# Two plain pairs instead of three at each feed forward entry, with the streams' sums made kind by kind

## The chip, the core and the metric

The kernel runs on one core of one Trainium2 chip. The metric is the device time of one execution in microseconds (us). The engines are named as in the profile: PE is TensorE (its weight loads are PEld), DVE is VectorE, ACT is ScalarE, POOL is GpSimd, SP is SyncE.

## The reference, cut to what matters

A decoder trunk of four layers works on 512 prompt tokens and 8 times 8 sample tokens. Each layer has a token mixer (attention, a gated recurrence, a short convolution, attention) and then a feed forward block:

```
xp = xp + swiglu(rmsnorm(xp, norm_ffn[i]), ffn_w_gate[i], ffn_w_up[i], ffn_w_down[i])
def swiglu(h, wg, wu, wd):
    return (jax.nn.silu(h @ wg) * (h @ wu)) @ wd
```

The model width is 1024 (8 row blocks of 128, numbered m or k), the feed forward width 2816 (22 column blocks of 128). All arithmetic is at float32 accuracy.

## The kernel before, in words

The 576 tokens are held transposed as two **streams** g = 0 and 1 of 288 columns each. A product at float32 accuracy is made of three matmuls over split operands: high weight times high data, high times low, low times high (`mm3`, lines 439 to 441). "Splitting" a tile is an ACT cast into the high part and a DVE subtraction for the low part: lines 412 and 414 (and 359 and 361) for weights, lines 468 and 470 for data. The split normed stream is `hh`, `hl`; the split input of the second matrix is `mh`, `ml`.

The 22 column blocks of a feed forward layer lie in three segments of 8, 7 and 7. In each segment the gate and up products of its blocks are made first, then the part of the down product (`out_units`) that they feed. A block's gate and up weights are a **pair**, and a pair is multiplied in one of two ways:

- **plain**: four units (gate and up, for both streams). A unit is 8 row blocks times 3 matmuls, so a plain pair is 96 matmuls. Its evacuation is a SiLU on ACT (line 1334) and a product on DVE (line 1343), then a data split.
- **quad** (`quad`): the two weights and the two streams are taken as a 2 by 2 block product with seven half-size products instead of eight. Each product is 4 row blocks times 3 matmuls (lines 1367 to 1369), so a quad is 84 matmuls. The products come in the order A11, A12, S2, S1, S3, S4, A22. A11 and A12 multiply the halves of stream 0; S4 the second half of stream 1; S2, S1, S3 and A22 multiply the data sums **T2, T1, T3 and T4**, which are sums of the halves of both streams. S3 can only add into its bank after a copy of the bank (`snap`, line 1375) has gone to a scratch tile, and S4 after another one.

The first `PRE` = 3 pairs of a layer are plain, since the data sums are not there yet; the five further pairs of the first segment and all of the other two are quads.

The **data sums** are made by `tsums(k)`, for k = 0 to 3, from blocks k and k+4 of both streams: five DVE operations (line 1322) and four data splits. Each `tsums(k)` first takes one scratch tile, and gives three back after its last split (`b12`, `b22` and its own). The scratch pool `scr` has `NSCR` = 10 tiles. `hsplit` (line 494 makes the normed block, then a split) takes one for each of the eight blocks of stream 1 and keeps it until `tsums` gives it back. The statistics of a stream (line 600), the SiLU tiles and the quads' copies take theirs from the same pool.

The **weight sums** of a quad (S1 to S4, lines 378, 381, 384 and 388) are made on DVE for the first `NEAR` = 2 quads of a layer and on POOL for the later ones; there is one set of sum tiles (`NSTP` = 1), which a quad holds until all its weights are split. `qprep` splits the seven weight halves one after the other into halves of `NSLOT` = 6 weight slots.

The order of the work on every engine is fixed when the program is built: `Sched` plays the tasks through with assumed costs, and on each engine takes the ready task of the lowest priority number (not an operation that is not ready yet). Priorities count in weight tiles. With i0 for the number of a layer's first gate weight: units of stream 0 have i0, i0+1, ...; units of stream 1 the same plus 3.5; a quad that begins at weight i has i + 1.75; a weight's split has i − 1 (each later half of a quad 2/7 more); a quad's weight sums i − 1.1; a stream's split that of its statistics (i0 + 2.5 for stream 1); `tsums(k)` has i0 + 2.6 + 0.1 k. Each stream has its own list of units, in which a unit begins only when the one before it has been issued; the quads go alternately into the two lists.

Of the kernel before, what the change touches and what calls it, by code (L numbers as in the profile page):

```python
# [14 lines left out]
D = 1024  # L15
# [3 lines left out]
T = 8  # L19
# [7 lines left out]
N = NP + NS  # L27
# [6 lines left out]
LAG = 3  # L34
NSLOT = 6
NRAW = 4
PRE = 3
NEAR = 2
NSTP = 1
TOFF = 2.6  # L40
# [209 lines left out]
def cD(n, ap=0):  # L250
    return n / 960 + 0.07 + 0.06 * ap


class Builder(Sched):
# [38 lines left out]
    def add(self, g, fn):  # L293
        self.units[g].append((self.vidx(g), fn))
        self.nunits[g] += 1
# [996 lines left out]
    def ffn(self, layer):  # L1292
# [7 lines left out]
        T = {}  # L1300
        mixed = self.mixed

        def enter():
            yield ("wait", mixed)
            self.open(f"{layer}f")
            for n in ("T2", "T1", "T3", "T4"):
                T[n] = tuple(self.lt(n + s, [P, hk, N], F32R) for s in "hl")
            self.stp = Pool([tuple(self.lt(f"S{j}{i}", [P, HW]) for j in range(2)) for i in range(NSTP)])
            self.b11 = [self.lt(f"b11{i}", [P, N]) for i in range(hk)]
            self.qseen = []  # L1310
            yield ("set", ("ffnlp", layer))

        def tsums(k):
            yield ("wait", [("h", g, idx, m) for g in range(2) for m in (k, k + hk)])
            b11, b12, b22 = (self.whole.pop(gm) for gm in ((0, k), (1, k), (1, k + hk)))
            hh, hl = (a[:, k + hk, :].bitcast(F32) for a in self.h[0])
            [t4] = yield ("acq", self.scr, 1)
            sub, add = nc.vector.tensor_sub, nc.vector.tensor_add
            for n, t, x, y, op in (("T1", b11, b12, b11, sub), ("T3", b12, b22, b12, sub), ("T2", b22, b22, b11, sub),
                                   (None, t4, hh, b22, sub), ("T4", t4, t4, hl, add)):  # L1320
                yield ("D", cD(N))
                op(t, x, y)

            def parts(n, t):
                yield from self.split(T[n][0][:, k, :], T[n][1][:, k, :], t, N, 1)
            for n, t in (("T1", b11), ("T3", b12), ("T2", b22), ("T4", t4)):
                yield ("spawn", parts(n, t), None, [("T", layer, n, k)])
            yield ("wait", [("T", layer, n, k) for n in ("T1", "T3", "T2", "T4")])
            yield ("free", self.scr, [b12, b22, t4])

        def gate_evac(g, key, ps):
            [t] = yield ("acq", self.scr, 1)
# [106 lines left out]
        def start_quad(prio, i, s, m, lst):  # L1439
            self.open_quads += 1  # L1440
            return quad(i, s, m, lst)

        self.spawn(enter(), 0.0, 0.0)
        for k in range(hk):
            self.spawn(tsums(k), self.nunits[1] + TOFF + 0.1 * k, 0.0)
        for s, (_, ns) in enumerate(SEGS):
            pre = PRE if s == 0 else 0
            for m in range(ns):
# [227 lines left out]
```

## Time and profile before

| | us |
|---|---|
| median of 3 runs | 2353.8 (2353.73 to 2353.94) |
| the profiled execution, its own time | 2353.24 |
| its span, first to last instruction | 2351.3 |
| PE busy | 2324.0 (99%) |
| DVE busy | 1672.2 (71%) |
| ACT busy | 1226.6 (52%) |
| POOL busy | 542.6 (23%) |

The span is what the views of the profile divide up. The profiled execution took 1.94 us more than its span, and stands 0.56 us below the median. In the views, times within the span are counted from its start, and a line such as L1322 is line 1322 of the kernel before.

### The profile page before, as it was taken

The numbers are of one execution on the slowest core, as the hardware profiler recorded it, in microseconds if no ns is written. First come the engines' busy times: TensorE is split into PE (matmuls) and PEld (weight loads), VectorE is DVE, ScalarE is ACT, GpSimd is POOL, SyncE is SP. The second block draws the span as 40 slices with busy tenths as digits, with TensorE's granted clock in tenths as the row PEclk, the third lists the DMA queues.
The fourth block names the chain that finished last, engine by engine and source line by source line (L and its number), as shares of the span: only waits on it lengthen the run. The fifth ranks groups of instructions, "written<-read, shape, count | busy, mean of one in ns | idle before, by whom it ended". The sixth has DMA issues, their size and how long they took to land.

```text
span 2351.3 us, 44296 instructions
## 1 busy us (share of the span) xinstructions
PE 2324.0 (99%) x17596; PEld 2295.5 (98%) x17596; DVE 1672.2 (71%) x3315; ACT 1226.6 (52%) x2545; POOL 542.6 (23%) x636
## 2 busy tenths in 40 slices
PE   9999999999999999999999999999999999999998
PEld 8899999999999999999999999999999899999998
DVE  8978848486886885848665578484868959757474
ACT  8955625255695653525422256252548945535353
POOL 2300334240231033323000003242402400333330
PEclk9999999999999999999999999999999999999999
DMA  5111323233222132323322213232242111323131
GB/s 189 61 57 47 112 87 99 73 101 102 72 82 93 52 122 66 113 72 101 97 85 82 83 55 98 93 98 81 88 138 83 56 46 54 126 73 110 62 109 49
DMA packets 64064, 203.69 MB, mean 87 GB/s; under 512 B 11041, under 2 KB 13905, under 8 KB 63841
## 3 DMA queue, kind: packets, MB, share of 16 engines
q1 hardware_dynamic: 62800, 199.52, 26.7%
q8 instruction: 138, 2.26, 0.4%
q10 hardware_dynamic: 720, 0.73, 0.1%
q0 software_dynamic: 336, 0.61, 0.1%
q14 instruction: 70, 0.57, 0.1%
HBM read 197.87 MB, written 4.94 MB: 86 GB/s over the span
## 4 chain that ended last, share of the span: by engine, by line
PE 86%; ACT 6%; DVE 4%; issue 2%; DMA 1%; POOL 0%; DVEq 0%; ACTq 0%
PE bank L439 16%; PE bank L440 16%; PE bank L441 16%; PE bank L1367 12%; PE bank L1369 12%; PE bank L1368 12%; ACT s L753 2%; ACT wh L359 1%; DVE P L841 1%; PE bank L890 1%; PE bank L906 1%; ACT P L847 0%; DVE P L855 0%; ACT PT L892 0%; DVE wl L361 0%
## 5 line engine op out<-in xcount | busy, mean ns | idle before, releaser
L439 PE MATMUL bank<-mh,wh 128*128 128x288 f32 x1984 | 589.2, 297 | 1.7 <-ACT mh L468 1.7
L440 PE MATMUL bank<-ml,wh 128*128 128x288 f32 x1984 | 586.0, 295 | 0.5 <-DVE ml L470 0.4
L441 PE MATMUL bank<-mh,wl 128*128 128x288 f32 x1984 | 583.7, 294 | 0.0
L439 PE MATMUL bank<-hh,wh 128*128 128x288 f32 x1344 | 404.1, 301 | 4.1 <-ACT s L1123 1.5
L440 PE MATMUL bank<-hl,wh 128*128 128x288 f32 x1344 | 397.3, 296 | 0.0
L441 PE MATMUL bank<-hh,wl 128*128 128x288 f32 x1344 | 396.3, 295 | 0.0
L414 DVE TENSOR_TENSOR wl<-raw,wh 128x512 fp32r<-128x512 f32 x380 | 375.9, 1011 | 22.8 <-ACT wh L412 22.6
L359 ACT CAST wh<-raw 128x1024 fp32r<-128x1024 f32 (+2 forms) x217 | 219.0, 1014 | 326.0 <-PE bank L440 213.1
L439 PEld LDWEIGHTS bank<-mh,wh 128*128 128x128 f32 x1984 | 371.9, 187 | 3.4 <-ACT mh L468 2.5
L440 PEld LDWEIGHTS bank<-ml,wh 128*128 128x128 f32 x1984 | 372.5, 188 | 1.8 <-DVE ml L470 1.3
L441 PEld LDWEIGHTS bank<-mh,wl 128*128 128x128 f32 x1984 | 373.7, 188 | 0.0
L361 DVE TENSOR_TENSOR wl<-raw,wh 128x1024 fp32r<-128x1024 f32 (+2 forms) x217 | 256.7, 1183 | 65.9 <-ACT wh L359 64.0
L655 DVE TENSOR_TENSOR x<-bank,x 128x288 f32<-128x288 f32 x224 | 101.9, 457 | 280.1 <-PE bank L441 279.9
L412 ACT CAST wh<-raw 128x512 fp32r<-128x512 f32 x380 | 229.5, 619 | 95.2 <-PE bank L440 94.6
L1367 PE MATMUL bank<-hh,wh 128*128 128x288 f32 x912 | 270.0, 296 | 0.0
L1368 PE MATMUL bank<-hl,wh 128*128 128x288 f32 x912 | 269.1, 295 | 0.0
L1369 PE MATMUL bank<-hh,wl 128*128 128x288 f32 x912 | 268.2, 294 | 0.0
L439 PEld LDWEIGHTS bank<-hh,wh 128*128 128x128 f32 x1344 | 252.5, 188 | 6.7 <-ACT s L1123 1.7
L440 PEld LDWEIGHTS bank<-hl,wh 128*128 128x128 f32 x1344 | 253.1, 188 | 0.8
L441 PEld LDWEIGHTS bank<-hh,wl 128*128 128x128 f32 x1344 | 253.7, 189 | 0.1
L1384 ACT ACTIVATE s<-s 128x288 f32<-128x288 f32 x152 | 67.8, 446 | 216.7 <-DVE s L1380 215.6
L1369 PEld LDWEIGHTS bank<-hh,wl 128*128 128x128 f32 x912 | 171.9, 188 | 0.0
(382 smaller groups left out, 4863.9 us busy)
## 6 DMA issues: line engine op xcount, KB each, us to landing
raw<-in_w SPq DMA_DIRECT2D x303, 512.0 KB
raw<-in_w SPq DMA_DIRECT2D x64, 448.0 KB
out_y<-x SPq DMA_DIRECT2D x12, 144.0 KB
x<-in_x SPq DMA_DIRECT2D x4, 288.0 KB
x<-in_x SPq DMA_DIRECT2D x2, 576.0 KB
ck<-in_ckt SPq DMA_DIRECT2D x4, 256.0 KB
cv<-in_cv SPq DMA_DIRECT2D x4, 256.0 KB
ca<-in_ca SPq DMA_DIRECT2D x2, 480.0 KB
```

Of the source, the lines that this page charges most:

```text
L359: self.nc.scalar.copy(fh[:, z], r[:, z])
L361: self.nc.vector.tensor_sub(fl[:, z], r[:, z], fh[:, z].bitcast(F32))
L412: self.nc.scalar.copy(fh, src)
L414: self.nc.vector.tensor_sub(fl, src, fh.bitcast(F32))
L439: mm(out, lhsT=wh(k), rhs=xh(k), start=(k == 0), stop=False)
L440: mm(out, lhsT=wh(k), rhs=xl(k), start=False, stop=False)
L441: mm(out, lhsT=wl(k), rhs=xh(k), start=False, stop=(k == n - 1))
L655: nc.vector.tensor_add(x[:, m, :], ps[:, :N], x[:, m, :])
L1367: mm(ps[:, :N], lhsT=wh[:, k, :], rhs=xh[:, k, :], start=first and k == 0, stop=False, skip_group_check=not first)
L1368: mm(ps[:, :N], lhsT=wh[:, k, :], rhs=xl[:, k, :], start=False, stop=False, skip_group_check=not first)
L1369: mm(ps[:, :N], lhsT=wl[:, k, :], rhs=xh[:, k, :], start=False, stop=k == hk - 1, skip_group_check=not first)
L1384: nc.scalar.activation(out=t, in_=t, func=AF.Silu)
```

## The change

`PRE` becomes 2, so that in each of the four layers the third pair is a quad; the first segment then has two plain pairs and six quads. In `tsums` the same five operations and four splits are issued in another order and with other priorities: T1 and T2 of a block first, and all work of a kind is ranked by kind (T2's splits, T1's, T3, T4) before it is ranked by block. The scratch tile is now taken for T2, and T4 is made in `b22`.

```diff
-PRE = 3
+PRE = 2
@@ tsums
-            [t4] = yield ("acq", self.scr, 1)
+            [t2] = yield ("acq", self.scr, 1)
             sub, add = nc.vector.tensor_sub, nc.vector.tensor_add
-            for n, t, x, y, op in (("T1", b11, b12, b11, sub), ("T3", b12, b22, b12, sub), ("T2", b22, b22, b11, sub),
-                                   (None, t4, hh, b22, sub), ("T4", t4, t4, hl, add)):
-                yield ("D", cD(N))
-                op(t, x, y)
+            rank = lambda z: tprio + 0.08 * z + 0.01 * k
...
-            for n, t in (("T1", b11), ("T3", b12), ("T2", b22), ("T4", t4)):
-                yield ("spawn", parts(n, t), None, [("T", layer, n, k)])
+            yield ("D", cD(N), rank(0))
+            sub(b11, b12, b11)
+            yield ("D", cD(N), rank(0))
+            sub(t2, b22, b11)
+            yield ("spawn", parts("T2", t2), 0.04, [("T", layer, "T2", k)])
+            yield ("spawn", parts("T1", b11), 0.08, [("T", layer, "T1", k)])
+            yield ("D", cD(N), rank(2))
+            sub(b12, b22, b12)
+            yield ("spawn", parts("T3", b12), 0.16, [("T", layer, "T3", k)])
+            yield ("D", cD(N), rank(3))
+            sub(b22, hh, t2)
+            yield ("D", cD(N), rank(3))
+            add(b22, b22, hl)
+            yield ("spawn", parts("T4", b22), 0.24, [("T", layer, "T4", k)])
             yield ("wait", [("T", layer, n, k) for n in ("T1", "T3", "T2", "T4")])
-            yield ("free", self.scr, [b12, b22, t4])
+            yield ("free", self.scr, [b12, b22, t2])
@@ ffn
+        tprio = self.nunits[1] + TOFF
         self.spawn(enter(), 0.0, 0.0)
         for k in range(hk):
-            self.spawn(tsums(k), self.nunits[1] + TOFF + 0.1 * k, 0.0)
+            self.spawn(tsums(k), tprio + 0.01 * k, 0.0)
```

## Rows read from the trace of the kernel before

**Rows 1.** The page: busy time by engine, and the chain that ended last.
```profile
PE 2324.0 (99%) x17596; PEld 2295.5 (98%) x17596; DVE 1672.2 (71%) x3315; ACT 1226.6 (52%) x2545; POOL 542.6 (23%) x636
...
PE 86%; ACT 6%; DVE 4%; issue 2%; DMA 1%; POOL 0%; DVEq 0%; ACTq 0%
```

**Rows 2.** Stretches of layer 0's entry: length, then busy PE, PEld, DVE, ACT, POOL, clock, DMA.
```profile
204.00:215.00 11.00, 11.00 (x83) 10.89 (x82) 7.84 (x21) 7.95 (x16) 0.00 (x0) 1.00 0.11 43
215.00:230.00 15.00, 15.00 (x115) 15.00 (x114) 14.52 (x37) 6.88 (x17) 0.00 (x0) 1.00 0.00 1
230.00:245.00 15.00, 15.00 (x114) 15.00 (x114) 13.77 (x29) 9.58 (x23) 0.00 (x0) 1.00 0.21 71
```

**Rows 3.** First start of T2's products and T1's first sums by layer, and T4's products.
```profile
L1367 PE MATMUL bank<-T2h_0f,wh x76: 295/296/297, 236.4 to 535.5; 128*128 128x288 f32 x76
...
L1367 PE MATMUL bank<-T4h_0f,wh x76: 293/296/398, 244.4 to 541.9; 128*128 128x288 f32 x76
...
L1367 PE MATMUL bank<-T2h_3f,wh x76: 295/296/298, 1988.5 to 2287.7; 128*128 128x288 f32 x76
...
L1322 DVE TENSOR_TENSOR b_0f<-s,b_0f x4: 450/452/453, 215.7 to 226.6; 128x288 f32<-128x288 f32 x4
...
L1322 DVE TENSOR_TENSOR b_3f<-s,b_3f x4: 451/452/455, 1967.9 to 1978.7; 128x288 f32<-128x288 f32 x4
```

**Rows 4.** Timeline of PE at layer 0's entry (start, us, instruction).
```profile
194.24 0.29 PE L439 MATMUL bank<-hh,wh 128*128 128x288 f32 x1
...
203.90 0.65 PE L600 MATMUL bank<-s,ones 128*128 128x288 f32 x2
204.17 0.51 PE L439 MATMUL bank<-hh,wh 128*128 128x288 f32 x1
...
229.96 0.30 PE L1367 MATMUL bank<-hh,wh 128*128 128x288 f32 x1
...
236.36 0.29 PE L1367 MATMUL bank<-T2h_0f,wh 128*128 128x288 f32 x1
```

**Rows 5.** Timeline of DVE at layer 0's entry.
```profile
206.80 0.46 DVE L613 SCALAR_TENSOR_TENSOR s<-bank,s 128x288 f32<-128x288 f32 x1 [2.74 <-ACT s L610]
...
208.14 1.37 DVE L494 SCALAR_TENSOR_TENSOR s<-x,cpack,rt 128x288 f32<-128x288 f32 x3
...
210.53 2.23 DVE L494 SCALAR_TENSOR_TENSOR s<-x,cpack,rt 128x288 f32<-128x288 f32 x5
213.07 1.94 DVE L470 TENSOR_TENSOR hl<-s,hh 128x288 fp32r<-128x288 f32 x5 [0.30 <-ACT hh L468]
214.92 0.45 DVE L470 TENSOR_TENSOR ml<-s,mh 128x288 fp32r<-128x288 f32 x1
...
217.70 0.46 DVE L1322 TENSOR_TENSOR s<-s,hl 128x288 f32<-128x288 f32 x1
...
219.05 0.45 DVE L470 TENSOR_TENSOR T1l_0f<-b_0f,T1h_0f 128x288 fp32r<-128x288 f32 x1
...
220.15 0.45 DVE L470 TENSOR_TENSOR T4l_0f<-s,T4h_0f 128x288 fp32r<-128x288 f32 x1
...
231.95 0.45 DVE L470 TENSOR_TENSOR T2l_0f<-s,T2h_0f 128x288 fp32r<-128x288 f32 x1
```

**Rows 6.** Timeline of ACT at layer 0's entry.
```profile
211.01 1.28 ACT L1334 ACT_TABLE_LOAD   x1 [1.03 <-PE bank L441]
...
220.70 0.41 ACT L1334 ACTIVATE s<-bank 128x288 f32<-128x288 f32 x1 [1.55 <-DVE T4l_0f L470]
```

**Rows 7.** Weight splits and weight sums by line: min/median/max ns, first and last start.
```profile
L414 DVE TENSOR_TENSOR wl<-raw,wh x380: 677/685/1802, 218.4 to 2278.1; 128x512 fp32r<-128x512 f32 x190
...
L378 POOL TENSOR_TENSOR S_0f<-raw x2: 1297/1304/1310, 247.4 to 258.7; 128x512 f32<-128x512 f32 x2
```

**Rows 8.** Stretches of layer 1 around a PE gap; columns as in rows 2.
```profile
706.00:709.50 3.50, 2.15 (x17) 1.92 (x15) 3.44 (x8) 3.47 (x6) 2.49 (x8) 1.00 0.00 0
709.50:712.00 2.50, 2.34 (x17) 2.34 (x18) 2.02 (x4) 2.48 (x7) 0.00 (x0) 1.00 0.16 29
```

## The prediction, made before the changed kernel was run

> **What bounds the kernel now.** I read the page's busy times and its chain first: PE is busy for 2324.0 of 2351.3 us, and 86% of the chain that ended last is PE's own work [rows 1]. So a matmul saved is worth its full pitch, and a wait is paid in full unless PE has other work in hand. Then I read the stretches of one feed forward entry: from 204 to 245 us PE has no idle time at all, while DVE is busy for 14.52 of 15 us from 215 to 230 [rows 2]. The reader should see there a PE without a gap beside a DVE without slack. The four entries are alike: from the first T1 sum to the first T2 product it is 236.4 − 215.7 = 20.7 us in layer 0 and 1988.5 − 1967.9 = 20.6 us in layer 3 [rows 3]. I therefore work one entry, layer 0's, and take it four times.
>
> **Term 1, matmuls removed.** A plain pair has 96 matmuls, a quad 84: 12 fewer in each layer, 48 in all. The pitch: between 229.96 and 236.36 us lie 48 matmuls (two quad products and a plain unit), 6.40 us, or 0.1333 us each [rows 4]. So −48 × 0.1333 = **−6.4 us**. If nothing waits, that is all that the change can give.
>
> The Trainium skill (TensorE: Matmul & The Clock Gate, "Wait — 56ns, not 53.3ns?") gives a warm start-to-start time of the columns over 2.4 GHz plus about 2.5 ns. For 288 columns that would be an estimated 122.5 ns, and the term 5.9 us, so the sum would come out 0.5 us higher. This kernel's row is 11 ns above that rule, and the row is used.
>
> **Term 2, the wait for stream 1's split.** Stream 1's statistics matmul stands at 203.90 us [rows 4]. Its split is a chain that nothing here shortens: DVE starts it at 208.14, after ACT's part, and its last subtractions begin at 213.07 and take 1.94 us, until 215.0 [rows 5]. Before, PE covers this with three plain units of stream 0, 72 matmuls × 0.1333 = 9.6 us from 204.17, until 213.8. With two pairs only one such unit is left. The quad behind it offers A11 and A12, 24 matmuls, and then needs T2; the quad after that is in the other list, behind stream 1's units. So cover falls to 48 matmuls = 6.4 us, until 210.6. Stream 1's first unit would end at 210.6 + 3.2 = 213.8 without a wait, but its last row block can begin only when the split ends. That is 215.0 as in the row, so the unit ends at 215.4: a wait of 1.6 us. Without the table load at 211.01 for the third pair's SiLU [rows 6], which holds the casts up, eight normings at 0.43 us (five take 2.23) and eight subtractions at 0.37 us (five take 1.94) end at 208.14 + 6.4 = 214.5 [rows 5]: a wait of 1.1 us. With the very last operations overlapping, 0.75 is the least I can get. I take 1.0, near the second value, since that table load goes: **+4.0 us** for four layers, ends 3.0 and 6.4.
>
> **Term 3, the data sums.** They must now be ready for T2 at 236.4 − 12.8 + 1.0 = 224.6 us (four plain units less, 96 × 0.1333, and the wait of term 2). The operations are the same 36. Splits follow each other every 0.37 us (219.05 to 220.15 is three steps); dependent sums every 0.49 us (215.7 to 217.70 is four steps) [rows 3, 5]. "Kind by kind over four blocks" is not what the scratch pool allows. Stream 1 holds 8 of 10 tiles, and the copy of A11 takes another one; four blocks would need 8 + 4 = 12. The trace before shows that this limit binds: a SiLU waits at 220.70 for the tile that the split at 220.15 returns [rows 5, 6], and the first sum starts just after the evacuation's split at 214.92. So block 0 goes alone, nine operations, about 4 us from 214.8, and its three tiles then let blocks 1 to 3 run kind by kind: six sums, 2.6 us, and three T2 splits, 1.1 us. T2 is ready at about 222.5, **2 us early**; T1 at 223.6, T3 at 225.8, both in time. But S3 has to wait for a copy that needs a scratch tile, and the first tile comes back when block 1's T4 is split: 218.8 plus 25 of the remaining operations at 0.37, some 228.0, and the copy takes 0.4. PE wants S3 at 224.6 + 3.2 = 227.8. That is a wait of 0.6 us; with the rate before (from 215.7 to 231.95 for all but one of the 36, 0.46 us each, other work included [rows 3, 5]) block 1 returns its tile at about 230.0, a wait of 2.6; with one that comes earlier, none. I take 0.7, nearer to the kind order that the diff writes: **+2.8 us**, ends 0 and 10.
>
> **Term 4, the quad's weight halves.** Seven splits of about 0.68 us and four DVE sums take the place of two splits of a whole tile. A11, A12, S2 and S1 fall in the 2.74 us in which DVE idles before 206.80 and in the room of the two tile splits [rows 5, 7]. The last three rank behind every data sum. They come in the gaps or after about 229.4 us, one cast and one split after another, some 1.3 us each, against 1.6 us for a product on PE. That just keeps up: I take 0.2 us, **+0.8 us**; ends 0 (all in gaps) and 2.0 a layer (all three after 229.4 and S4 wanted at 229.4), which is 8 us.
>
> Costed at nothing: the added bank copies and adds of a quad (hidden beside PE, with DVE at 71%; without that cover they would be four operations of 0.45 us a layer), and the gaps' effect on the clock. After the gap near 708 us, where PE was busy for 2.15 of 3.50 us, the granted clock is still 1.00, the 2.4 GHz level [rows 8].
>
> **Sum.** −6.4 + 4.0 + 2.8 + 0.8 = +1.2 us against the profiled execution's own 2353.24: 2354.4. The median stands 0.56 higher, so 2355.0 against 2353.8. A measurement of this kernel tells a difference of about 0.2%, or 4.7 us, from none: **no change**, with waits that eat the saving.
>
> **The rivals.**
> - *Nothing waits.* Term 1 alone: 2353.8 − 6.4 = 2347.4. For it: PE has no gap at the entry now. Against it: term 2's chain, whose start is fixed by a matmul that the change leaves where it is. If term 2 alone remains it is 2350.4, and not to be told from no change.
> - *Weight halves late (slower).* Place: S4, A22 and the next quads' first halves, in the 10 us after the data sums. It decides from the point where the halves come more than 1.6 us apart. For it: DVE has under 0.5 us in 15 to spare there [rows 2], and POOL's first weight sums, now at 247.4 [rows 7], move up to about 236, into this catching up. Price: a split that runs beside POOL takes up to 1.80 us instead of 0.68 [rows 7]; two of them and one late sum are 2.9 us a layer, less the 0.2 counted. 2355.0 + 4 × 2.7 = 2365.8. Against it: the later quads run with POOL's sums without PE waiting.
> - *Sums no faster than before (slower).* If the tiles let the blocks go only one at a time, the last T2 split comes 231.95 − 215.7 = 16.3 us after the first sum, as before [rows 3, 5]: done at 214.8 + 16.7 = 231.5 against 224.6, a wait of 6.9 instead of 0.7 us a layer. 2355.0 + 4 × 6.2 = 2379.8. Against it: block 0 returns three tiles at once, just enough.
>
> **How the numbers follow.** Forecast 0.55, nothing waits 0.12, weight halves late 0.23, sums no faster 0.06; 0.04 is left for a slower case that I don't see. Only the first rival is faster by over 0.2%: 0.12. The forecast's own range is 2350.4 (term 2 at its low end, the others nil) to 2358, within 0.2%: 0.55. Slower: 0.33. The 8-in-10 range leaves out the last two cases, and most of the first: 2349.5 to 2366.0.
>
> **What would show it.** 48 matmuls fewer; at each entry, some 6.4 us after the statistics matmul, a PE gap of about 1 us in the first unit of stream 1, ended by the split's DVE or ACT lines; T2's first product at about 224.6 us without a wait; a short wait before T3's product, ended by the bank copy; the T1 sums of blocks 1 to 3 together, behind block 0's last split. A PE with no gap at the entries would make terms 2 to 4 wrong; gaps before T2, S4 or the third quad would bear out the slower rivals.

## The result and the profile after

The changed kernel takes 2380.9 us (median of 4 runs, 2379.96 to 2381.83) against 2353.8: 1.0116 times the time before, with an interval of 1.0103 to 1.0129. It is slower by 27 us, where no change was forecast. The page of the changed kernel, its busy times and its chain:

```profile
PE 2335.6 (98%) x17548; PEld 2292.6 (96%) x17548; DVE 1700.7 (72%) x3347; ACT 1244.3 (52%) x2579; POOL 565.5 (24%) x652
...
PE 82%; DVE 11%; ACT 4%; issue 1%; DMA 1%; POOL 0%; DVEq 0%; ACTq 0%
```

Against [rows 1], PE has its 48 matmuls less (17596 to 17548), and DVE's share of the chain went from 4% to 11%. The windows of layer 0's entry, with the columns of [rows 2], show where:

```profile
204.00:215.00 11.00, 9.82 (x69) 8.93 (x67) 8.59 (x21) 7.54 (x17) 0.00 (x0) 1.00 0.01 2
215.00:230.00 15.00, 13.73 (x102) 13.50 (x102) 14.76 (x39) 9.06 (x22) 0.00 (x0) 1.00 0.00 1
230.00:245.00 15.00, 14.57 (x103) 13.80 (x104) 14.48 (x26) 8.72 (x20) 4.20 (x3) 1.00 0.25 70
```

PE, which had no idle time there, now issues 274 matmuls in these 41 us in place of 312. DVE is a little fuller than before (14.76 us against 14.52 in the second stretch). The timeline of PE of the changed kernel in layer 0 (start, duration, instruction, and in brackets the idle time ahead of it and what ended it; L1376 to L1378 are now the quads' matmuls, L1384 the copy of a bank):

```profile
203.38 0.65 PE L600 MATMUL bank<-s,ones 128*128 128x288 f32 x2
...
210.25 0.29 PE L439 MATMUL bank<-hh,wh 128*128 128x288 f32 x1
...
211.81 0.40 PE L439 MATMUL bank<-hh,wh 128*128 128x288 f32 x1 [0.20 <-ACT hh L468]
212.57 0.40 PE L440 MATMUL bank<-hl,wh 128*128 128x288 f32 x1 [0.37 <-DVE hl L470]
...
214.91 0.40 PE L440 MATMUL bank<-hl,wh 128*128 128x288 f32 x1 [0.31 <-DVE hl L470]
...
225.28 0.29 PE L1376 MATMUL bank<-T2h_0f,wh 128*128 128x288 f32 x1
...
229.90 0.40 PE L1376 MATMUL bank<-T3h_0f,wh 128*128 128x288 f32 x1 [1.27 <-ACT s L1384]
...
235.58 0.41 PE L1378 MATMUL bank<-hh,wl 128*128 128x288 f32 x1 [0.35 <-DVE wl L414]
...
251.21 0.40 PE L1378 MATMUL bank<-T2h_0f,wl 128*128 128x288 f32 x1
251.44 0.29 PE L1376 MATMUL bank<-T2h_0f,wh 128*128 128x288 f32 x1
...
262.79 0.40 PE L1378 MATMUL bank<-T2h_0f,wl 128*128 128x288 f32 x1
...
586.25 0.65 PE L600 MATMUL bank<-s,ones 128*128 128x288 f32 x2
```

The first and the last row give the measure used from here on: from stream 1's statistics at the entry to the next layer's first statistics, 586.25 − 203.38 = **382.87 us**. Before, with 203.90 from [rows 4] and this row of PE, it is 581.52 − 203.90 = 377.62, the same in layers 0 to 2:

```profile
581.52 0.65 PE L600 MATMUL bank<-s,ones 128*128 128x288 f32 x2
```

What PE waited is what the steps between two starts have over the 0.1333 us of a matmul. In the changed kernel a wait mostly costs one slow step more: the next matmul starts 0.23 to 0.24 us behind the late one (251.21 and 251.44). In layer 0 the waits are 2.2 us for stream 1's split (211.8 to 215.2), 1.5 before T3's product, 1.5 around the second quad (235.6 to 246.3), and 0.39 in the T2 product of each of the four quads after it (251.21, 262.79 and two more): 1.6. Together that is 6.8, less the 1.6 saved, 5.2 a layer; the four layers (5.25, 5.12, 5.13, 5.25) make 20.8 us.

The rest is a place where the diff does nothing. Layer 3's attention, from stream 1's statistics to the next one, takes 1957.40 − 1797.24 = 160.16 us where it took 153.92: +6.2. PE of the changed kernel, then of the kernel before:

```profile
1797.24 0.65 PE L600 MATMUL bank<-s,ones 128*128 128x288 f32 x2
...
1922.66 0.41 PE L940 MATMUL bank<-ca,P 128*128 128x128 f32 x2 [1.52 <-DVE P L855]
...
1957.40 0.65 PE L600 MATMUL bank<-s,ones 128*128 128x288 f32 x2
```

```profile
1782.44 0.65 PE L600 MATMUL bank<-s,ones 128*128 128x288 f32 x2
...
1936.35 0.65 PE L600 MATMUL bank<-s,ones 128*128 128x288 f32 x2
```

The planner wrote another order of the same instructions there, with the output units made in one block ahead of this row, so that nothing covers the wait of 1.52 us for DVE. Behind it and a second wait, of 0.36 us, PE's granted clock falls to 0.50, the 1.2 GHz level, for 6.8 us; in the attention of the kernel before it is 1.00 throughout. Run e1 below has PE's matmuls in the order of the changed kernel there, with the same two waits, and keeps 1.00. The windows of the changed kernel and of e1, with the columns of [rows 2]:

```profile
1923.40:1930.20 6.80, 6.53 (x32) 4.60 (x33) 4.67 (x19) 4.04 (x16) 0.00 (x0) 0.50 0.00 0
```

```profile
1936.15:1942.95 6.80, 5.05 (x46) 3.65 (x48) 4.90 (x21) 5.01 (x19) 0.00 (x0) 1.00 0.00 1
```

e1's attention takes 158.7 us, and that of e9, with the same order and a clock of 1.00 as well, 158.9. So of the 6.2 us some 4.9 are the order by itself and 1.2 to 1.5 the slow clock. In all 20.8 + 6.2 = 27.0; the start and the other mixers give back 0.7, and the end takes 0.6 more, near the 26.8 by which the two spans differ (2378.1 and 2351.3).

### The profile page after: what moved, and what is told of

Same layout as the page of the kernel before. It is cut to its first block, busy times and chain, and to the rows that moved or that the text cites. A ratio compares the mean times of both kernels' runs of the same rounds, so it can differ in the third digit from the quotient of the medians.

```text
span 2378.1 us, 44301 instructions
## 1 busy us (share of the span) xinstructions
PE 2335.6 (98%) x17548; PEld 2292.6 (96%) x17548; DVE 1700.7 (72%) x3347; ACT 1244.3 (52%) x2579; POOL 565.5 (24%) x652
## 4 chain that ended last, share of the span: by engine, by line
PE 82%; DVE 11%; ACT 4%; issue 1%; DMA 1%; POOL 0%; DVEq 0%; ACTq 0%
PE bank L439 16%; PE bank L441 15%; PE bank L440 15%; PE bank L1378 11%; PE bank L1376 11%; PE bank L1377 11%; DVE ml L470 2%; ACT s L753 2%; DVE wl L414 2%; PE bank L890 1%; PE bank L906 1%; ACT P L847 1%; DVE wl L361 1%; DVE hl L470 1%; DVE P L841 0%
## 5 line engine op out<-in xcount | busy, mean ns | idle before, releaser
L414 DVE TENSOR_TENSOR wl<-raw,wh 128x512 fp32r<-128x512 f32 x400 | 394.8, 1006 | 30.8 <-ACT wh L412 30.7
L359 ACT CAST wh<-raw 128x1024 fp32r<-128x1024 f32 (+2 forms) x209 | 210.6, 1011 | 316.7 <-PE bank L440 199.8
L439 PE MATMUL bank<-hh,wh 128*128 128x288 f32 x1216 | 367.3, 302 | 4.5 <-DVE ext L1086 2.4
L440 PE MATMUL bank<-hl,wh 128*128 128x288 f32 x1216 | 360.3, 296 | 2.7 <-DVE hl L470 2.7
L441 PE MATMUL bank<-hh,wl 128*128 128x288 f32 x1216 | 358.5, 295 | 0.0
L361 DVE TENSOR_TENSOR wl<-raw,wh 128x1024 fp32r<-128x1024 f32 (+2 forms) x209 | 248.2, 1189 | 63.7 <-ACT wh L359 61.9
L412 ACT CAST wh<-raw 128x512 fp32r<-128x512 f32 x400 | 241.1, 618 | 95.4 <-PE bank L440 94.9
L1378 PE MATMUL bank<-hh,wl 128*128 128x288 f32 x960 | 283.6, 295 | 1.4 <-DVE wl L414 1.4
L1376 PE MATMUL bank<-hh,wh 128*128 128x288 f32 x960 | 284.1, 296 | 0.0
L1377 PE MATMUL bank<-hl,wh 128*128 128x288 f32 x960 | 283.2, 295 | 0.0
L439 PEld LDWEIGHTS bank<-hh,wh 128*128 128x128 f32 x1216 | 228.7, 188 | 9.3 <-ACT hh L468 3.9
L440 PEld LDWEIGHTS bank<-hl,wh 128*128 128x128 f32 x1216 | 229.1, 188 | 5.0 <-DVE hl L470 4.4
L441 PEld LDWEIGHTS bank<-hh,wl 128*128 128x128 f32 x1216 | 229.6, 189 | 0.2 <-DVE wl L361 0.2
L1378 PEld LDWEIGHTS bank<-hh,wl 128*128 128x128 f32 x960 | 180.8, 188 | 2.9 <-DVE wl L414 2.3
```

What stands on the lines that cost most here:

```text
L359: self.nc.scalar.copy(fh[:, z], r[:, z])
L361: self.nc.vector.tensor_sub(fl[:, z], r[:, z], fh[:, z].bitcast(F32))
L412: self.nc.scalar.copy(fh, src)
L414: self.nc.vector.tensor_sub(fl, src, fh.bitcast(F32))
L439: mm(out, lhsT=wh(k), rhs=xh(k), start=(k == 0), stop=False)
L440: mm(out, lhsT=wh(k), rhs=xl(k), start=False, stop=False)
```

## The experiments

"Layer" is the measure above, the mean of layers 0 to 2; "attention" that of layer 3. A run's ratio is to runs of the kernel before that were taken beside it.

| run | us | ratio to before | layer | attention |
|---|---|---|---|---|
| before | 2353.8 | | 377.6 | 153.9 |
| after | 2380.9 | 1.0103 to 1.0129 | 382.8 | 160.2 |
| e1 | 2394.3 | 1.0159 to 1.0190 | 386.7 | 158.7 |
| e2 | 2352.4 | 0.9987 to 1.0006 | 377.6 | 154.0 |
| e3 | 2375.0 | 1.0077 to 1.0107 | 382.8 | 154.2 |
| e4 | 2383.2 | 1.0112 to 1.0142 | 383.7 | 159.9 |
| e5 | 2373.4 | 1.0068 to 1.0102 | 382.4 | 154.0 |
| e6 | 2381.4 | 1.0101 to 1.0131 | 384.3 | 155.2 |
| e7 | 2392.0 | 1.0149 to 1.0179 | 382.2 | 159.2 |
| e8 | 2379.3 | 1.0094 to 1.0125 | 379.1 | 159.2 |
| e9 | 2387.4 | 1.0131 to 1.0161 | 385.4 | 158.9 |
| e10 | 2360.3 | 1.0017 to 1.0039 | 379.4 | 153.7 |
| e11 | 2376.1 | 1.0083 to 1.0117 | 382.7 | 154.2 |
| e12 | 2356.3 | 1.0002 to 1.0022 | 378.3 | 154.0 |
| e13 | 2362.2 | 1.0023 to 1.0053 | 379.8 | 153.7 |
| e14 | 2384.1 | 1.0116 to 1.0146 | 383.8 | 160.3 |
| e15 | 2376.2 | 1.0084 to 1.0114 | 381.6 | 160.2 |
| e16 | 2369.3 | 1.0053 to 1.0083 | 382.6 | 154.0 |
| e17 | 2351.0 | 0.9980 to 1.0000 | 377.6 | 154.0 |

**The two parts of the change, one at a time.** e1 has two plain pairs with the sums of before; e2 has three plain pairs with the new sums.

```diff
 e1: PRE = 2, tsums and its priorities as before
 e2: PRE = 3, tsums and its priorities as after
```

> Only PRE = 2, with the data sums made as before, block by block. Theory A (the order of the sums matters, and what the changed kernel waits for are three things at each entry: the split of stream 1, the scratch tile for a bank copy, the weight halves): T2's last split comes about 16 us after the first sum instead of 8, so PE waits some 6 us before T2's first product, gets back the 1.5 us wait before T3 and about 1 us of the weight waits; net about +4 us a layer, 2381 + 16 = about 2397. Rival B (the sums are not on the path, their order is nothing): 2381 within 2.

> Three plain pairs as before, with the sums in the new order. Theory A: PE has no gap at the entries of the kernel before, so nothing is to be gained or lost: 2353.8 within 1.5, no PE gap at the entries. Rival: the new order is itself slower (its sums leave the other DVE work no room): above 2356, with gaps at the entries.

With the old sums PE waits in the T2 product itself. PE of e1 in layer 0:

```profile
229.23 0.40 PE L1368 MATMUL bank<-T2l_0f,wh 128*128 128x288 f32 x1 [1.71 <-DVE T2l_0f L470]
...
232.66 0.61 PE L1368 MATMUL bank<-T2l_0f,wh 128*128 128x288 f32 x1 [1.82 <-DVE T2l_0f L470]
```

The new sums take these waits away, which is worth 13.4 us (2394.3 to 2380.9); with three plain pairs they change nothing that can be measured. So the loss is that of the smaller `PRE`. The 13.4 us are not the waits alone: near these places of e1, in all four layers, PE's clock falls to 0.50 for a while, and some 70 matmuls start 0.24 us apart; in the layers of the changed kernel it stays at 1.00.

**Layer 3's attention.** e3 sets the planner's assumed clocks 1.5 us on at that attention and leaves the work as it is.

```diff
+            if layer == 3:
+                for e in self.t:
+                    self.t[e] += 1.5
```

> The changed kernel with one line that puts the planner's assumed clocks forward by 1.5 us when layer 3's attention begins; no instruction is added, and PE's order in that attention becomes that of the kernel before. Theory A (6.2 us of the loss are another order that the planner chose for layer 3's attention): 2381 - 6 = about 2375, the four feed forward layers unchanged. Rival C (the attention is late because the feed forward before it hands on late weights or transfers): 2381 within 1.5.

The attention falls back to 154.2 us, the layers stay at 382.8, and the time falls by 6.0 us: that part of the loss hangs on the order, the slow clock included, which with the order of before doesn't come.

**Waits taken away one by one.** e4 makes the weight sums of six quads on DVE; e5 gives the first quad's copy ahead of S4's product a tile of its own; e6 makes T4's two sums on POOL; e11 does both e5 and e6.

```diff
 e4
-NEAR = 2
+NEAR = 6
 e5, snap (its lines that make `own` and give the tile back are not shown)
-                [c[n]] = yield ("acq", self.scr, 1)
+                [c[n]] = yield ("acq", self.own if n == 2 and s == 0 and m == PRE else self.scr, 1)
 e6, tsums
-            yield ("D", cD(N), rank(3))
-            sub(b22, hh, t2)
-            yield ("D", cD(N), rank(3))
-            add(b22, b22, hl)
+            yield ("G", 0.75)
+            nc.gpsimd.tensor_sub(b22, hh, t2)
+            yield ("G", 0.75)
+            nc.gpsimd.tensor_add(b22, b22, hl)
```

> The changed kernel with the weight sums of all six quads of the first segment on DVE (NEAR = 6) and not on POOL from the third on. Theory A (the repeated waits of 0.4 us before each later quad's T2 product come from the POOL sums, which begin only when the quad before has given back its sum tiles): these four waits a layer go, about -1.6 us a layer, 2381 - 6 = about 2375. Rival D (DVE is what is short; four more operations of 0.7 us a quad make it worse): 2381 or more, with longer waits for weight splits.

> The changed kernel with one more scratch tile that only the second bank copy of a layer's first quad may take. The measure is the time from stream 1's statistics matmul at an entry to the next statistics matmul: 377.6 us before the change, 382.8 after it. Theory A (the 1.5 us wait before T3's first product is for a scratch tile): that wait goes; a part of it, up to 1 us, comes back as a longer wait for the weight halves behind it, so 381.3 to 382.3. Rival (T3's product waits for its data sum or its weights): 382.8 and the wait stays. The planner's order of layer 3's attention becomes that of the kernel before, which alone is worth 6 us in all: in all about 2371 to 2375 by theory A, 2375 by the rival.

> The changed kernel with T4's two sums of each block on POOL, which is idle there, and not on DVE: eight operations of 0.37 to 0.49 us a layer less on DVE in the stretch where it has no slack. Measure as before (382.8 us after the change). Theory A (DVE is what is short between the split and the second quad): the waits for weight halves of the first two quads, about 1.3 us a layer, shrink, and the scratch tiles come back no sooner, so 381.5 to 382.5. Rival E (POOL's sums of two SBUF tiles hold up DVE's, or are themselves too slow at about 0.75 us each): 383 or more, with a longer wait before T3's or T4's first product.

> The changed kernel with both earlier edits together: T4's two sums of each block on POOL (8 DVE operations, about 3 us, less a layer), and a scratch tile of its own for the copy ahead of the first quad's S4, so that neither DVE's sums nor the pool of tiles stands before T3's product. Theory (DVE's queue is what PE waits for, the tile only the place where the wait shows): DVE has 3 us less to do, of 6.8 us of waits about 4 are left, among them 2.2 for stream 1's split: interval 380 us a layer, time about 2370 with layer 3's attention in its other order. Rival (the sums on POOL are late whatever the tiles do, and the one long wait before T3's product stays): 384 us a layer, time 2381 as with the sums on POOL alone.

None of them frees a layer of its waits. e4 and e6 come out as their rivals said, slower by 0.9 and 1.5 us a layer, and e5 just past its theory's range (382.4, not 382.3 at most). DVE of e4 in layer 0:

```profile
245.25 0.45 DVE L1389 TENSOR_TENSOR s<-s,bank 128x288 f32<-128x288 f32 x1 [1.62 <-PE bank L1378]
...
248.15 0.68 DVE L414 TENSOR_TENSOR wl<-raw,wh 128x512 fp32r<-128x512 f32 x1
```

DVE stands idle for 1.62 us ahead of L1389, which needs a product of PE, and the next quad's weight split comes five operations later, at 248.15, behind another split and three weight sums: the wait of each later quad is now in its first product (0.58 us instead of 0.42). In e5 the wait before T3's product is gone, and the one for the second quad's weights has grown from 0.64 us between two starts to 1.35; the sum of layer 0's waits stays 6.9. (The 0.4 us that the layer gains come evenly in the matmuls far behind the entry, at no wait.) Of its gain of 7.6 us, 6.2 are layer 3's attention, back in the order of before. PE of e5, then of e6:

```profile
234.59 0.40 PE L1378 MATMUL bank<-hh,wl 128*128 128x288 f32 x1 [1.05 <-DVE wl L414]
```

```profile
233.77 0.40 PE L1376 MATMUL bank<-T3h_0f,wh 128*128 128x288 f32 x1 [4.06 <-ACT s L1384]
```

In e6 the sums on POOL are late, and PE stands before T3's product for 4.06 us; behind it no matmul of layer 0's later quads waits any more. But PE's clock is 0.50 behind that wait, and 14 matmuls start 0.24 us apart: 1.5 us by themselves, as much as e6 loses a layer against the changed kernel. e11 halves the wait (2.04 us idle), but 13 matmuls are slow in the same way and the second quad waits again: 382.7, the value of neither theory.

**The planner's assumed cost of a matmul.** Three matmuls take 0.40 us in the trace and 0.369 in the planner; e7 (after) and e8 (before) tell it 0.4.

```diff
-            yield ("P", 0.369 * (e - k), None, None, 864 * (e - k))
+            yield ("P", 0.4 * (e - k), None, None, 864 * (e - k))
...
-                yield ("P", 0.369 * hk, None, None, 864 * hk)
+                yield ("P", 0.4 * hk, None, None, 864 * hk)
```

> The changed kernel planned with the cost of a PE step that the trace shows (0.400 us for three matmuls where the planner takes 0.369). Same instructions, other order. Theory F (a good part of the waits is the planner's order, made for a PE that is 8% too fast, so that DVE work stands in the queue behind things that come later than assumed): the repeated waits of 0.4 us of the later quads go, 1.6 us a layer, 381.2 or less instead of 382.8. Rival (they are real lateness of the weights): 382.8 within 0.5.

> The kernel before, planned with the same measured PE cost. Its feed forward layers have no waits, so 377.6 stays; only the attention layers' order can move the time: 2353.6 within 6 either way.

Both miss: the truer number makes both kernels slower, by 11 and 25 us. In e7 layers 0 to 2 gain 0.6 on average (0.1, −0.4 and 2.0) and the rest loses: the first statistics come 4.7 us later, the 21.3 us between the first statistics of the mixer behind layer 0 and the second become 24.1, and layer 3 loses 3.1. In e8 the same places lose, the layers 1.2 to 4.9 each, and layer 3's attention 5.3.

**More work on DVE, known to the planner.** e9 (after) and e10 (before) have one idle subtraction more for each block of the data sums; the lines are e9's, and e10's has no rank.

```diff
+            yield ("D", cD(N), rank(0))
+            sub(self.spare, b12, b11)
```

> The changed kernel with one more subtraction on DVE for each of the four data-sum blocks of a layer, written into a spare tile that nobody reads: 4 x about 0.37 = 1.5 us of DVE time a layer, at the rank of the T1 and T2 sums. Theory (behind stream 1's split DVE has no slack until the second quad's weights are split, so that whatever DVE has to do there PE waits for): the interval between the statistics matmuls of a feed forward layer goes from 382.8 to about 384.3 us, and the time up by about 6 us, to 2387, if the attention of layer 3 keeps its order. Rival (each wait has its own cause, a scratch tile, the split, a late weight half, and DVE's throughput sets none of them): the interval moves by less than 0.5 us, time 2381 to 2383.

> The kernel before with the same four dummy subtractions a layer. Theory (with three plain pairs the work on PE covers DVE's entry, so DVE's extra work there costs nothing): the interval of a feed forward layer stays at 377.6 us within 0.5 us; the time differs only by what another order of layer 3's attention costs (about +6 us, since the planner's order there is another one in this kernel: about 2360). Rival (DVE is the bound in the kernel before already): 377.6 + 1.5 = 379.1 a layer, 6 us more in all.

e9 seems to speak for the theory that DVE has no slack, with more than it asked for (2.6 us a layer, not 1.5). But behind its longer wait before T3's product (3.25 us) PE's clock falls to 0.50 in every layer, and 13 to 24 matmuls start 0.24 us apart, which is 1.4 us of it and more. And e10 goes to the rival: 1.8 us a layer in the kernel before too, at a clock of 1.00. In e10, though, most of the waits are not at the data sums; they are the 0.42 us steps in each later quad's T2 product, as in the changed kernel. That could be the work or the other order, and the next four runs keep one of the two fixed.

**Order and work apart.** e12 (before) and e14 (after) have the dummies without telling the planner, so each engine keeps its order; e13 (before) tells the planner of dummies that aren't there; e15 (after) leaves out T4's two sums behind the planner's back, so that T4 is stream 1's second block alone.

```diff
 e12, e14
+            sub(self.spare, b22, b12)
 e13
+            yield ("D", cD(N))
 e15
-            sub(b22, hh, t2)
-            add(b22, b22, hl)
```

> The kernel before with the four dummy subtractions a layer on DVE, but unknown to the planner, so that every engine keeps the order of the kernel before. Theory O (the order that the planner writes decides whether PE waits; at the entry of the kernel before DVE has some 1.5 us to spare): interval 377.6 to 378.2 us, time within 2 us of before. Theory D (DVE's time at the entry is the bound, and the kernel before stands exactly at it): interval 379.1 to 379.5, time +6 to +7.5 us, 2360.

> The kernel before with nothing added, but the planner told of four more DVE operations a layer at the data sums: the order of the run with the dummies that the planner knew of, without their work. Theory O: the waits of about 0.42 us before the later quads' T2 products stay, interval about 379 us, time about 2359. Theory D: DVE's work is that of before, so the interval falls back to about 377.6, and the time differs by layer 3's attention alone (that kernel's was 153.69 us against 153.92, so nothing): 2353 to 2354.

> The changed kernel with the four dummy subtractions a layer unknown to the planner: order of the changed kernel, 1.5 us more of DVE's time at each entry. Theory D (no slack on DVE there): interval 382.8 + 1.5 = 384.3 us, time 2387. Theory O: under 0.7 us more a layer, time at most 2384.

> The changed kernel without T4's two sums of each block (T4 is made of the second block of stream 1 alone; eight DVE operations, some 3 us a layer, left out), unknown to the planner: order as in the changed kernel. Theory D: 3 us less of DVE's time, of the 6.8 us of waits 2.2 for stream 1's split stay and of the other 4.6 some 1.6 to 2: interval about 380 us, time about 2370. Theory O (the order sets the waits): the wait before T3's product goes, 1.5 us, the recurring ones stay: interval about 381.3 us, time about 2375.

In the kernel before the order counts more than the work, and neither theory holds alone. In e13, with no work added, a layer costs 2.2 us more, in waits that the changed kernel has as well: around one quad and in the T2 product of the later ones. The waits for stream 1's split and before T3's product e13 doesn't have. DVE and then PE of e13 in layer 0:

```profile
257.72 0.68 DVE L414 TENSOR_TENSOR wl<-raw,wh 128x512 fp32r<-128x512 f32 x1
258.32 1.92 DVE L470 TENSOR_TENSOR ml<-s,mh 128x288 fp32r<-128x288 f32 x2
260.16 0.68 DVE L414 TENSOR_TENSOR wl<-S_0f,wh 128x512 fp32r<-128x512 f32 x1
```

```profile
260.90 0.41 PE L1370 MATMUL bank<-T2h_0f,wl 128*128 128x288 f32 x1
```

S2's split (`wl<-S_0f`) stands behind A12's split and the two output splits of the quad before, and the matmul that needs it starts as it ends. DVE of the kernel before, and of the changed one:

```profile
256.13 1.16 DVE L414 TENSOR_TENSOR wl<-S_0f,wh 128x512 fp32r<-128x512 f32 x1
257.20 0.81 DVE L470 TENSOR_TENSOR ml<-s,mh 128x288 fp32r<-128x288 f32 x2
```

```profile
259.61 0.68 DVE L414 TENSOR_TENSOR wl<-raw,wh 128x512 fp32r<-128x512 f32 x1
260.21 1.92 DVE L470 TENSOR_TENSOR ml<-s,mh 128x288 fp32r<-128x288 f32 x2
262.06 0.68 DVE L414 TENSOR_TENSOR wl<-S_0f,wh 128x512 fp32r<-128x512 f32 x1
```

Before, S2's split comes ahead of the output splits, and nothing waits; after, it is the order of e13. The work counts for about half of itself or less: 1.5 us more on DVE costs 0.7 a layer in e12 and 0.9 in e14 (1.24, 0.57, 1.24, 0.58; the clock falls in the first three of these layers, so 0.58 is the one without it), and 3 us less gives back 1.2 in e15, where just the wait before T3's product goes and the recurring ones stay. PE of e12 and of e14, layer 0:

```profile
231.97 0.40 PE L1371 MATMUL bank<-hh,wl 128*128 128x288 f32 x1 [0.83 <-DVE wl L414]
```

```profile
232.01 0.47 PE L1377 MATMUL bank<-T3h_0f,wh 128*128 128x288 f32 x1 [2.25 <-ACT s L1385]
```

So the kernel before has under 1 us a layer to spare at its entry: of 1.5 us more, 0.7 are paid.

**The other order in the changed kernel.** Ranking the weights' work 0.3 of a tile earlier gives the later quads of layer 0 the order of before; e16 is after, e17 before.

```diff
-PREP = 1
+PREP = 1.3
```

> The changed kernel with PREP = 1.3 in place of 1, so that the planner ranks the weights' splits and sums 0.3 of a weight tile earlier. The order then written for the later quads of the first segment is the one that the kernel before has there (both halves of a weight ahead of the other quad's output splits; S2's split ahead of them), and layer 3's attention has the order of before again; the work is the same. Theory O (the order alone makes the recurring waits of 0.39 us before the later quads' T2 products): they go, 4 x 0.39 = 1.6 us a layer, some 0.7 more goes with the gaps of 0.1 us beside the second quad, the waits for stream 1's split (2.2) and before T3's product (1.5) stay: interval 380.5 to 381.3 us, attention about 154, time 2366 to 2370. Theory D (DVE's time is the bound and the order only the place where it shows): interval 382.3 to 383, time about 2375.

> The kernel before with the same PREP = 1.3, as a control: its later quads have that order already and nothing waits, so interval 377.6 us and attention 153.9 as before, time within 2 us of before by either theory.

DVE and PE of e16 in layer 0:

```profile
259.64 1.15 DVE L414 TENSOR_TENSOR wl<-S_0f,wh 128x512 fp32r<-128x512 f32 x1
260.72 0.82 DVE L470 TENSOR_TENSOR ml<-s,mh 128x288 fp32r<-128x288 f32 x2
```

```profile
235.24 0.40 PE L1378 MATMUL bank<-hh,wl 128*128 128x288 f32 x1 [1.59 <-DVE wl L414]
```

The recurring waits of layer 0 are gone, but the wait for the second quad's weights has grown from 0.64 to 1.89 us between two starts, and the layer gains 1.2, less than the 1.5 to 2.3 of the theory of the order. Layers 1 and 3 lose 1.7 and 0.8: there the later quads wait before T3's product. The 11.7 us that e16 gains lie in layer 3's attention (6.2) and the mixer between layers 0 and 1 (4.1). The theory of the order explains where these waits stand, not that a layer could do without them; which order would, if any, stays open. The control e17 keeps its layers at 377.6; it takes 2.7 us less than before where at most 2 were expected, 1.7 of them in the mixer between layers 0 and 1. That is the fastest of the runs, and with a ratio of up to 1.0000 it beats the kernel before by hardly more than a measurement can tell.

## Why the prediction was wrong

The forecast was 2355.0, and it is 2380.9. Three terms of the sum were too small, and a fourth place had no term.

**Term 1 held.** 48 matmuls went.

**Term 2 was mis-sized**: 1.0 us forecast, 2.2 measured. The unit starts at 210.25 as forecast (210.6). What failed is "I take 1.0 ..., since that table load goes": the split ends no sooner without it. ACT of the kernel before, then ACT and DVE of the changed kernel at the entry:

```profile
204.58 1.28 ACT L608 ACT_TABLE_LOAD   x1
```

```profile
203.94 0.61 ACT L412 CAST wh<-S_0f 128x512 fp32r<-128x512 f32 x1
204.57 1.28 ACT L608 ACT_TABLE_LOAD   x1
...
208.90 0.40 ACT L1384 COPY s<-bank 128x288 f32<-128x288 f32 x1 [0.26 <-PE bank L1378]
```

```profile
208.10 1.37 DVE L494 SCALAR_TENSOR_TENSOR s<-x,cpack,rt 128x288 f32<-128x288 f32 x3
209.67 1.20 DVE L470 TENSOR_TENSOR hl<-s,hh 128x288 fp32r<-128x288 f32 x3 [0.20 <-ACT hh L468]
...
214.04 0.45 DVE L470 TENSOR_TENSOR ml<-s,mh 128x288 fp32r<-128x288 f32 x1
214.40 0.82 DVE L470 TENSOR_TENSOR hl<-s,hh 128x288 fp32r<-128x288 f32 x2
```

The cast of the new quad's S half, one of the edits that term 4 looked at on DVE alone, stands on ACT ahead of the statistics' table load, which starts 1.19 us behind the statistics matmul instead of 0.68. The normings begin at 208.10, 4.7 us behind the statistics matmul instead of 4.2. From there to the end it takes 7.1 us, not the 6.4 of the forecast: the first subtractions wait 0.20 us for casts that stand on ACT behind the quad's bank copy (costed at nothing), and an output split goes ahead of the last two. They end at 215.2, 11.8 us behind the statistics matmul where it was 11.1. The value taken was the second, and even the upper end (1.6) was too low. No run moves the cast or the copy, so their shares are read from these rows and not shown by an experiment.

**Term 3 was right in its mechanism, and a size was off.** T2's first product stands at 225.28 without a wait (forecast 224.6, from a start 0.5 us later), and the T1 sums of blocks 1 to 3 go together behind block 0's last split, as foreseen. The wait before T3's product is 1.5, not 0.7. DVE and ACT of the changed kernel:

```profile
228.40 0.45 DVE L470 TENSOR_TENSOR T4l_0f<-s,T4h_0f 128x288 fp32r<-128x288 f32 x1
```

```profile
228.86 0.70 ACT L1343 ACTIVATE s<-bank 128x288 f32<-128x288 f32 x2
229.45 0.70 ACT L1384 COPY s<-bank 128x288 f32<-128x288 f32 x2
```

The split at 228.40 gives the tile back at 228.85 (forecast 228.0), and two SiLUs that wait for tiles as well go ahead of the copy: they were not in the step.

**Term 4 failed**: 0.2 us forecast, 3.0 measured (1.5 around the second quad, 1.6 recurring). "That just keeps up" priced each half by its duration and let it come in its turn. It left out that the planner would write the order in which the halves stand behind other work for every later quad, so that the loss recurs. The rival "weight halves late" had the first of these places and almost this price, 2.9 us a layer; it was given 0.23. The slow splits beside POOL that it reckons with are there (two weight splits at 240.92 take 3.34 us), but no run shows what they alone cost. The rival "sums no faster" comes nearest to the measured time with 2379.8, but by chance: its place, T2's first product, has no wait.

**The sum** with the measured terms: −6.4 + 4 × (2.2 + 1.5 + 3.0) = +20.4, near the 20.8 of the layers. The three waits were each taken well below their upper ends, 1.6, 2.6 and 2.0 us, which together are 6.2 and near the 6.8 measured, and they were added as if independent. They are not: the runs in which one wait was taken away (e5, e16) show it again at the next operation in the queue. And layer 3's attention, 6.2 us, had no term: the forecast took all of the program outside the entries as unchanged. The gaps' effect on the clock, put at nothing from one gap that left it at 1.00, is nothing in the four layers but 1.2 to 1.5 us of these 6.2.

## What to carry to other kernels

Where one engine has no gap and the engine that feeds it no slack, work taken off the first can come back as waits for the second: price the feeder's whole queue over that stretch, not the waits one by one. Where a planner writes the order, a small edit can reorder stages far from it; hold the order fixed (work that the planner isn't told of, or costs without work) before a difference is put down to the edit itself. Look at the granted clock of each run, too, before a wait is priced by the difference of two times.

## What was not expected of the hardware

PE's clock did not go by the length of a wait alone. In e14 PE waits 2.25 us before T3's product in layers 0, 2 and 3. Behind that wait the clock falls in layers 0 and 2 and stays at 1.00 in layer 3. The windows of e14 behind the wait in layer 2 and in layer 3 (length, busy PE, PEld, DVE, ACT, POOL, clock, DMA):

```profile
1423.50:1426.80 3.30, 3.30 (x16) 3.30 (x15) 3.26 (x8) 2.20 (x5) 0.00 (x0) 0.50 0.58 171
2008.70:2012.00 3.30, 3.30 (x25) 3.30 (x26) 3.30 (x8) 2.91 (x7) 0.00 (x0) 1.00 0.47 134
```

0.50 is the 1.2 GHz level, with 16 matmuls where the other level has 25. In layer 1 of e14 it falls behind the four waits for stream 1's split, 0.21 to 0.36 us each, which left it at 1.00 in every layer of the changed kernel. It stayed at 1.00 behind 1.27 idle us in the changed kernel and 1.59 in e16, and it fell behind 1.52 and 0.36 in layer 3's attention. What decides is not shown here.

Two output splits on DVE take 1.92 us instead of 0.81 where a weight sum of POOL runs beside them; before, that sum (255.36 to 256.74) runs beside S2's split, which takes 1.16 us instead of 0.68. So the order also decides which of the two is held up. POOL of the changed kernel:

```profile
260.44 1.38 POOL L388 TENSOR_TENSOR raw<-raw,S_0f 128x512 f32<-128x512 f32 x1 [3.55 <-DVE wl L414]
```
